# RWKV time mixing on one core: second products of the receptance mix on GpSimd

## The chip, the cores and the metric

The kernel runs on one core of a Trainium2 chip. A core has five engines that run their own instruction queues side by side and meet only at semaphores: TensorE (PE, with its weight loads listed as PEld), VectorE (DVE), ScalarE (ACT), GpSimd (POOL) and SyncE (SP, here only a queue for DMAs). The metric is the device time of one execution in microseconds (us); the figure that counts is the median over several executions. A profile is one execution recorded instruction by instruction. Its span runs from the first to the last instruction and is a little shorter than the time of the same execution.

## What is computed

x has the shape 16 x 2048 x 256 (batch, sequence, channels); all weights are 256 x 256. Cut to what matters:

```python
x_prev[:, 1:, :] = x[:, :-1, :]
xv = x * time_mix_v + x_prev * (1 - time_mix_v)
xr = x * time_mix_r + x_prev * (1 - time_mix_r)
v = xv @ value_weight
r = xr @ receptance_weight
out = ((1 / (1 + np.exp(-r))) * v) @ output_weight
```

The key path of the reference is computed there but not used in its output, and the kernel leaves it out.

## The kernel before

**Tiles.** The 16 x 2048 tokens are cut into 64 units of 512 tokens; four units make a batch entry. x is loaded by DMA from POOL's queue, converted to bf16 (`load`, L103 to L118), and turned by TensorE so that channels lie on the partitions (`transposes`, L197); ACT copies the turned tile from PSUM into `xt` (L225). A tile has 2 halves of channels (`ko` 0 and 1), and each half of a unit has 512 columns. The batch entries 0 and 1 are held unit by unit in `xt_first`; from entry 2 on, `xt` holds the entry as a whole.

**The mix.** With the factor (1 - tm)/tm held in `c_sb`, and tm itself multiplied into the weights, a mix is `c * x_prev + x`. It is made per unit and per m, where m = 0 is R (receptance) and m = 1 is V (value), each called a piece. A piece takes two products, one for each channel half, and one sum over both:

- `scale` (L255) makes a product on DVE (L258, 128 x 512 for one unit, 128 x 1024 for two).
- `scale_pool` (L266) makes the second product (`ko` = 1) on POOL (L268). A dependency written by hand holds it until a given DVE sum is done.
- `scale_act` (L512) makes a product on ACT (L515).
- `add` (L278) makes the sum on DVE (L280, 128 x 1024).

The column of x before a unit's first is not in its own slot; `wrap_slots` (L412) copies it there once per unit or batch entry, by two small copies (L427, L428), before the first product that reads it.

**The main loop** (L523) makes one step per unit g, in this order on the engines: TensorE projects R of unit g (`project`, L288, into psum_r), ACT takes the sigmoid (L536), TensorE transposes units further ahead, DVE makes the products and sums that are due in this step, TensorE projects V (L288, into psum_v), DVE multiplies sigmoid and V into `z_sb` (L581), POOL makes its products, DVE makes the sums that are held back until after z, and TensorE multiplies z of the step before by the output weight (L312, into psum_o), which ACT copies out (L346) and SP's queue stores. psum_r, psum_v and psum_o have one buffer each. The order is written out by hand; no scheduler moves anything.

**Which engine makes which product** is decided in a planning loop (L499 to L510) ahead of the main loop. For each piece, `products[w]` says what DVE makes in step w, and `pooled[w - 1]` which pieces' second product POOL makes in the step before. Before the change, units 10 and later are taken in pairs, and POOL makes the second product of both R and V. Of units 3 to 8 POOL makes the second product of V only; unit 9 has all four on DVE. Unit 1's V product is on POOL and unit 2's second V product on ACT (L563). `AHEAD` is 6 and `PAIRS` is 10. Up to unit 7, a unit's R sum stands in the step before its projection, ahead of z; unit 8's R sum stands after z of step 6. The lines that place POOL's work in a step:

```python
        for p in pooled[g]:                    # L587, after z of step g
            wrap_slots(p, after=last)          # last: the last DVE sum ahead of z
            scale_pool(p, last)
        for p in held[g]:                      # L590
            add(p)
```

So a step's POOL queue holds one wrap copy (L428) and one product, then, where one is due, the issue of a load (L114), and the small copy (L427) of a unit further on.

Of the kernel before, what the change touches and what calls it, by code (L numbers as in the profile page):

```python
# [15 lines left out]
def kernel(  # L16
# [45 lines left out]
    AHEAD = 6  # L62
    PAIRS = 10
# [15 lines left out]
    SYNC = mybir.DependencyInfo(mybir.DependencyClass.Sync, mybir.DependencyReason.DATA)  # L79
# [164 lines left out]
    def slots(piece, off=0):  # L244

        b, _, lo, hi = piece
        j = lo // P + (lo // TU if b < BYUNIT else 0) + off
        return slice(j, j + (hi - lo) // P)

    def mixed(piece):  # L250
        b, m, lo, hi = piece
        j = lo // P % (2 * UJ)
        return mix[(b * S + lo) // (2 * TU)][:, m, j : j + (hi - lo) // P]
# [9 lines left out]
                op0=ALU.mult,  # L263
            )

    def scale_pool(piece, after):  # L266
        b, m, _, _ = piece
        op = nc.gpsimd.tensor_scalar(  # L268
            out=mixed(piece)[:, :, 1],
            in0=xt[b][:, slots(piece), 1],  # L270
            scalar1=c_sb[:, m, 1:2],
            scalar2=1.0,
            op0=ALU.mult,
            op1=ALU.mult,
        )
        tc.add_manual_dep(op.ins, after.ins.name, SYNC, reason="one at a time")

    def add(piece):  # L278
        b = piece[0]
        return nc.vector.tensor_tensor(  # L280
            out=mixed(piece), in0=mixed(piece), in1=xt[b][:, slots(piece, 1)], op=ALU.add
        )
# [13 lines left out]
    def project_unmixed(ps, mo):  # L296


        parts = [(w_prev[:, ko], ko, 0) for ko in range(KO)]
        parts += [(w_bf[:, 0, ko], ko, 1) for ko in range(KO)]  # L300
        for n, (w, ko, lo) in enumerate(parts):
            nc.tensor.matmul(  # L302
                out=ps[:, mo, :],
                lhsT=w[:, mo * P : (mo + 1) * P],
                rhs=xt[0][:, lo : lo + UJ, ko],
                start=(n == 0),
                stop=(n == len(parts) - 1),
            )
# [92 lines left out]
    def tile_for(b):  # L401

        if b not in mix:
            mix[b] = mixpool.tile([P, 2, 2 * UJ, KO, P], BF16, name="mix")

    def pieces(g):

        b, e = divmod(g, UB)
        tile_for(g // 2)
        return [(b, m, e * TU, (e + 1) * TU) for m in range(2)]  # L410

    def wrap_slots(piece, one=None, after=None):  # L412


        b, _, lo, _ = piece
        by_unit = b < BYUNIT
        key = (b, lo // TU if by_unit else UB - 1)
        if key not in late_copies:
            return
        kos = slice(0, KO) if one is None else slice(one, one + 1)  # L420
        if one in (None, KO - 1):
            late_copies.remove(key)
        j = slots(piece).start if by_unit else 0
        n = UJ if by_unit else J
        if by_unit and j > 0:
            engine = nc.vector if key == (0, 1) else nc.gpsimd
            engine.tensor_copy(out=xt[b][:, j, kos, 0:1], in_=xt[b][:, j - 1, kos, P - 1 : P])  # L427
        op = (nc.vector if after is None else nc.gpsimd).tensor_copy(  # L428
            out=xt[b][:, j, kos, 1:P], in_=xt[b][:, j + n, kos, 0 : P - 1]
        )  # L430
        if after is not None:
            tc.add_manual_dep(op.ins, after.ins.name, SYNC, reason="one at a time")
# [4 lines left out]
    def advance(limit):  # L437
        nonlocal tnext, half_load, last_load
        while tnext <= min(limit, NU - 1):
            b, e = divmod(tnext, UB)  # L440
            if b == 1 and e > 0:
                load(b + e + 1)
            elif b > 1 and e == 0 and b + 5 < B:
                if b == 2:
                    load(6)
                last_load = load(b + 5)
                if b + 5 == B - 1:
                    half_load, last_load = last_load
            if tnext < NU - BYDMA:
                transposes(tnext)  # L450
            tnext += 1
# [34 lines left out]
    pooled = {g: [] for g in range(-1, NU)}  # L486
# [12 lines left out]
    for u in range(2, NU):  # L499
        paired = u >= PAIRS  # L500
        if paired and u % 2:
            continue
        for m, (b, _, lo, hi) in enumerate(pieces(u)):
            w = first[u][m]
            group = (b, m, lo, hi + TU if paired else hi)
            if paired or m == 1 and w > 1 and u != PAIRS - 1:
                products[w].append((group, (0,)))
                pooled[w - 1].append(group)
            else:
                products[w].append((group, (0,) if u == 2 and m == 1 else (0, 1)))  # L510

    def scale_act(piece, kos):  # L512
        b, m, _, _ = piece
        for ko in kos:
            nc.scalar.activation(  # L515
                out=mixed(piece)[:, :, ko],
                in_=xt[b][:, slots(piece), ko],
                func=ACT.Copy,
                scale=c_sb[:, m, ko : ko + 1],
            )  # L520

    z_prev2 = z_prev = None
    for g in range(NU - 1):  # L523
        ps_r = ps_r_pool.tile([P, KO, TU], FP32, name="psum_r")
        if g == 0:
            project_unmixed(ps_r, 0)
            advance(1)
            project_unmixed(ps_r, 1)
            for ko in range(KO):
                wrap_slots(pieces(1)[0], ko)  # L530
                scale(pieces(1)[0], (ko,))
            last = add(pieces(1)[0])
        else:
            project(ps_r, g, 0)
        s_sb = zpool.tile([P, KO, TU], BF16, name="s_sb")
        nc.scalar.activation(out=s_sb, in_=ps_r, func=ACT.Sigmoid)  # L536
        advance(START_T[g] if g < len(START_T) else g + LOOK - (g == CROSS - 1))
        for b in range(B - 5, B):
            if g == max(UB * (b - 2) - 1, CROSS + (b > B - 5)):
                new_xt(b)  # L540
                if b == B - 5:
                    for pair in kept.pop(g):
                        store(nc.sync, *pair, after=half_load)
                    by_dma(b, J - UJ, J, last_load)
                    by_dma(b, 0, J - UJ, last_load)
                else:
                    by_dma(b, 0, J)
                for pair in kept.pop(g, []):
                    store(nc.sync, *pair)
            if g == UB * (b - 1) + 1:  # L550
                nc.scalar.copy(out=xt[b][:, 0, :, 1:P], in_=xt[b][:, J, :, 0 : P - 1])
        if LATE_O < g < NU - 2:
            output(g - 2, z_prev2)
        for p in products.get(g + 1, []):
            if g >= FREE and p[0][1] == 1:
                scale_act(p[0], (0,))
        for p in [q for q, _ in products[g]] + pooled[g]:
            last_unit_of = p[3] // TU - 1
            need = last_unit_of if p[0] < BYUNIT else min(last_unit_of + 1, UB - 1)
            assert UB * p[0] + need < tnext, (g, p, tnext)  # L560
            if g > AHEAD or p not in pooled[g]:
                wrap_slots(p)
        if g == 1:  # L563
            scale_act(pieces(2)[1], (1,))
        for p, kos in products[g]:
            if not (g - 1 >= FREE and p[1] == 1):
                scale(p, kos)
        for p in sums[g]:
            last = add(p)
        for p in pooled[g]:  # L570
            if p[0] >= BYUNIT:
                wrap_slots(p)
        ps_v = ps_v_pool.tile([P, KO, TU], FP32, name="psum_v")
        project(ps_v, g, 1)
        if g == 0:
            scale_act(pieces(1)[1], (0,))
            advance(2)
        z_sb = zpool.tile([P, KO, TU], BF16, name="z_sb")
        n = TU // 2 if g == NU - 2 else TU
        for c in range(0, TU, n):  # L580
            nc.vector.tensor_tensor(  # L581
                out=z_sb[:, :, c : c + n],
                in0=s_sb[:, :, c : c + n],
                in1=ps_v[:, :, c : c + n],
                op=ALU.mult,
            )
        for p in pooled[g]:  # L587
            wrap_slots(p, after=last)
# [3 lines that stand above are left out]
        if z_prev is not None and not LATE_O <= g < NU - 3:  # L592
            output(g - 1, z_prev)
        if g == 1:
            advance(4)
        z_prev2, z_prev = z_prev, z_sb
# [31 lines left out]
```

## Time and profile before

| what | value |
|---|---|
| median of 9 runs | 202.75 us (202.41 to 205.46) |
| the profiled execution: its time | 202.58 us |
| the profiled execution: its span | 200.5 us |
| POOL product L268, 128 x 512, mean (6 of xt_first) | 685 ns |
| POOL wrap copy L428, mean | 393 ns |
| DVE product L258, 128 x 512, mean (22 of xt_first) | 349 ns |
| DVE sum L280, mean | 697 ns |
| DVE z L581, mean | 1200 ns |
| ACT product L515, first two (10.75 and 14.24 us) | 0.71 and 0.73 us |
| granted TensorE clock | 0.999 of full |

The page of a profile lists the busy time of each engine, the chain of work that ended last, and the costliest groups by line. A mean is the recorded length of one instruction; on DVE the next one can start before that length is over, so that three products of 349 ns take 0.88 us from the first start to the last end and 0.80 us to the start of what follows. The first 35 us of the span are where single units are used; after that, POOL's product of a pair (128 x 1024) takes 1.1 us.

### The profile page before, as it was taken

Reading aid. Unit: us, or ns where it says so; the run is one execution under the profiler, and the core shown is the slowest. Engines: PE = TensorE matmul, PEld = TensorE weight load, DVE = VectorE, ACT = ScalarE, POOL = GpSimd, SP = SyncE. Lnnn points to the kernel's source line nnn. Section 1 sums busy time; section 2 is a strip of 40 time slices with the busy share of each in tenths; the row PEclk is TensorE's granted clock in tenths of the full one; section 3 lists DMA queues with packets and bytes.
Section 4 is the critical chain, followed back from the end, with each engine's and each line's share of the span. In section 5 each row is a group of like instructions: output and inputs, shape, how many; then the busy total and the mean of one; then the engine's idle time right before and its main releaser. Section 6 shows DMA issues by size and latency. Waiting matters only on the chain.

```text
span 200.5 us, 3886 instructions
## 1 busy us (share of the span) xinstructions
PE 195.0 (97%) x1420; PEld 125.6 (63%) x1420; DVE 186.2 (93%) x296; ACT 180.1 (90%) x202; POOL 83.7 (42%) x115
## 2 busy tenths in 40 slices
PE   8899999999999999999999999999999999999993
PEld 7575676666666666666666666655666565555671
DVE  2799999999999999999999999999999999999982
ACT  3599899999999999999999999899999999999982
POOL 1746572443543534425433354443344444444200
PEclk9999999999999999999999999999999999999999
DMA  5999999999999999999999999999999999999575
GB/s 171 292 167 214 231 280 272 280 282 274 290 314 288 286 280 288 291 273 284 288 286 335 296 412 283 290 176 206 293 270 394 345 220 273 414 420 405 237 310 213
DMA packets 32298, 57.26 MB, mean 286 GB/s; under 512 B 21780, under 2 KB 23064, under 8 KB 28312
## 3 DMA queue, kind: packets, MB, share of 16 engines
q1 hardware_dynamic: 28208, 40.77, 59.3%
q0 software_dynamic: 3920, 16.12, 40.0%
q8 instruction: 11, 0.18, 0.3%
q10 hardware_dynamic: 152, 0.13, 0.2%
q14 instruction: 7, 0.06, 0.1%
HBM read 34.34 MB, written 33.55 MB: 339 GB/s over the span
## 4 chain that ended last, share of the span: by engine, by line
PE 86%; DVE 5%; DMA 3%; issue 2%; ACT 2%; SPq 1%; POOL 0%; DVEq 0%
PE psum_v L288 26%; PE psum_o L312 25%; PE psum_r L288 24%; PE ps_t L209 9%; DMA o_sb<-in_x_dram 3%; DVE z_sb L581 2%; DVE mix L280 2%; PE ps_t L312 1%; DVE mix L258 1%; ACT s_sb L536 1%; ACT mix L515 1%; ACT xt L225 1%; PE ps_t L288 0%; PE psum_r L302 0%; SPq L128 0%
## 5 line engine op out<-in xcount | busy, mean ns | idle before, releaser
L268 POOL TENSOR_SCALAR mix<-xt,c_sb 128x1024 bf16<-128x1024 bf16 (+1 forms) x55 | 61.0, 1109 | 92.6 <-DVE mix L280 79.3
L581 DVE TENSOR_TENSOR z_sb<-s_sb,psum_v 128x1024 bf16<-128x1024 bf16 (+1 forms) x64 | 76.7, 1200 | 3.6 <-PE psum_v L288 1.5
L280 DVE TENSOR_TENSOR mix<-mix,xt 128x1024 bf16<-128x1024 bf16 x112 | 77.0, 697 | 1.6
L288 PEld LDWEIGHTS <-w_bf 128*128 128x128 bf16 x516 | 48.7, 98 | 38.6 <-issue 0.7
L536 ACT ACTIVATE s_sb<-psum_r 128x1024 bf16<-128x1024 f32 x63 | 65.0, 1031 | 3.5 <-PE psum_r L288 2.7
L346 ACT COPY o_sb<-psum_o 128x1024 f32<-128x1024 f32 x60 | 61.1, 1018 | 7.1 <-PE psum_o L312 7.1
L288 PE MATMUL psum_v<-mix,w_bf 128*128 128x512 bf16 (+1 forms) x256 | 65.3, 377 | 0.3 <-DVE z_sb L581 0.2
L288 PE MATMUL psum_r<-mix,w_bf 128*128 128x512 bf16 (+1 forms) x252 | 64.2, 377 | 0.1
L312 PE MATMUL psum_o<-wo_bf,z_sb 128*128 128x256 bf16 x486 | 63.2, 273 | 0.0
L312 PEld LDWEIGHTS <-z_sb 128*128 128x128 bf16 x512 | 49.8, 98 | 20.4 <-issue 1.4
L225 ACT COPY xt<-ps_t 128x1024 bf16<-128x1024 bf16 x36 | 36.6, 1030 | 0.0
L209 PEld LDWEIGHTS <-x_bf 128*128 128x128 bf16 x328 | 21.5, 98 | 8.8
L209 PE MATMUL ps_t<-ident,x_bf 128*128 128x128 bf16 x328 | 24.5, 219 | 0.0
L258 DVE TENSOR_SCALAR mix<-xt,c_sb 128x1024 bf16<-128x1024 bf16 (+1 forms) x49 | 22.1, 459 | 0.0
L515 ACT ACTIVATE mix<-xt,c_sb 128x1024 bf16<-128x1024 bf16 x12 | 13.9, 1157 | 0.0
L280 DVE TENSOR_TENSOR mix<-mix,xt_first 128x1024 bf16<-128x1024 bf16 x15 | 10.6, 709 | 0.1
L114 POOL DMA_DIRECT2D x_bf<-in_x_dram x13 | 8.6, 661 | 0.0
L258 DVE TENSOR_SCALAR mix<-xt_first,c_sb 128x512 bf16<-128x512 bf16 x22 | 6.6, 349 | 0.2
L225 ACT COPY xt_first<-ps_t 128x1024 bf16<-128x1024 bf16 x5 | 5.2, 1036 | 0.0
L268 POOL TENSOR_SCALAR mix<-xt_first,c_sb 128x512 bf16<-128x512 bf16 x6 | 4.1, 685 | 0.9 <-DVE mix L280 0.4
L428 POOL COPY xt_first<-xt_first 128x254 bf16<-128x254 bf16 x5 | 2.0, 393 | 5.5 <-DVE mix L280 5.4
L153 PE MATMUL ps_t<-zeros 128*128 128x128 bf16 x31 | 3.2, 284 | 1.0 <-DVE zeros L90 1.0
(66 smaller groups left out, 51.4 us busy)
## 6 DMA issues: line engine op xcount, KB each, us to landing
out_dram<-o_sb SPq DMA_DIRECT2D x28, 1024.0 KB, 14.1
x_bf<-in_x_dram POOLq DMA_DIRECT2D x13, 1024.0 KB, 23.4
out_dram<-o_sb SPq DMA_DIRECT2D x4, 512.0 KB, 2.8
out_dram<-o_sb SPq DMA_DIRECT2D x6, 256.0 KB, 2.5
x_bf<-in_x_dram POOLq DMA_DIRECT2D x5, 256.0 KB, 7.0
o_sb<-in_x_dram SPq DMA_DIRECT2D x2, 512.0 KB, 5.5
x_bf<-in_x_dram POOLq DMA_DIRECT2D x2, 512.0 KB, 10.8
o_sb<-in_x_dram SPq DMA_DIRECT2D x2, 256.0 KB, 2.8
```

What stands on the lines that cost most here:

```text
L114: return nc.gpsimd.dma_start(out=x_bf[b], in_=rows(b), max_dma_last_dim=run)
L209: nc.tensor.transpose(out=ps[:, jj], in_=src[:, jj, ko * P : (ko + 1) * P], identity=idn)
L225: nc.scalar.copy(out=xt[b][:, j0 : j0 + UJ], in_=ps)
L258: nc.vector.tensor_scalar(out=mixed(piece)[:, :, ko], in0=xt[b][:, slots(piece), ko], scalar1=c_sb[:, m, ko : ko + 1], scalar2=None, op0=A ...
L268: op = nc.gpsimd.tensor_scalar(out=mixed(piece)[:, :, 1], in0=xt[b][:, slots(piece), 1], scalar1=c_sb[:, m, 1:2], scalar2=1.0, op0=ALU.mul ...
L280: return nc.vector.tensor_tensor(out=mixed(piece), in0=mixed(piece), in1=xt[b][:, slots(piece, 1)], op=ALU.add)
L288: nc.tensor.matmul(out=ps[:, mo, :], lhsT=w_bf[:, m, ko, mo * P : (mo + 1) * P], rhs=mixed((b, m, e * TU + lo, e * TU + hi))[:, :, ko], st ...
L312: nc.tensor.matmul(out=ps[:, slot, :], lhsT=z[:, ko, jj * P : (jj + 1) * P], rhs=wo_bf[:, ko, :], start=(ko == 0), stop=(ko == KO - 1),)
L346: nc.scalar.copy(out=o_sb[b][:, j0 : j0 + UJ, :], in_=ps)
L515: nc.scalar.activation(out=mixed(piece)[:, :, ko], in_=xt[b][:, slots(piece), ko], func=ACT.Copy, scale=c_sb[:, m, ko : ko + 1],)
L536: nc.scalar.activation(out=s_sb, in_=ps_r, func=ACT.Sigmoid)
L581: nc.vector.tensor_tensor(out=z_sb[:, :, c : c + n], in0=s_sb[:, :, c : c + n], in1=ps_v[:, :, c : c + n], op=ALU.mult,)
```

## The change

R's pieces of units 3 to 8 are treated as V's: DVE makes the first product, POOL the second. In POOL's list R's piece comes ahead of V's, so that the wrap copy comes with R's. For unit 8 both POOL products stand in step 6, and its wrap copy stays on DVE. The second V product of unit 2 goes from ACT to POOL, in step 1, without the dependency on a DVE sum. Unit 9 and the pairs are as before.

```diff
-    def scale_pool(piece, after):
+    def scale_pool(piece, after=None):
         b, m, _, _ = piece
         op = nc.gpsimd.tensor_scalar(
...
-        tc.add_manual_dep(op.ins, after.ins.name, SYNC, reason="one at a time")
+        if after is not None:
+            tc.add_manual_dep(op.ins, after.ins.name, SYNC, reason="one at a time")
...
-            if paired or m == 1 and w > 1 and u != PAIRS - 1:
+            if paired or w > 1 and u != PAIRS - 1:
                 products[w].append((group, (0,)))
-                pooled[w - 1].append(group)
+                at = w if m == 0 and u == AHEAD + 2 else w - 1
+                pooled[at].insert(0 if m == 0 else len(pooled[at]), group)
             else:
                 products[w].append((group, (0,) if u == 2 and m == 1 else (0, 1)))
...
-            if g > AHEAD or p not in pooled[g]:
+            if g > AHEAD or p not in pooled[g] or p == pieces(AHEAD + 2)[0]:
                 wrap_slots(p)
         if g == 1:
-            scale_act(pieces(2)[1], (1,))
+            scale_pool(pieces(2)[1])
```

## The prediction

> **What bounds the kernel now.** I read the page's shares and chain first, then a table of windows cut at the first weight load of each step's R projection, then the timeline of DVE and POOL. "Step g" is one turn of the main loop, "unit u" the 512 tokens projected in step u; R and V are the two mixes of a unit.
>
> ```profile
> PE 195.0 (97%) x1420; PEld 125.6 (63%) x1420; DVE 186.2 (93%) x296; ACT 180.1 (90%) x202; POOL 83.7 (42%) x115
> PE 86%; DVE 5%; DMA 3%; issue 2%; ACT 2%; SPq 1%; POOL 0%; DVEq 0%
> ```
> TensorE carries the end for most of the span, POOL for none. DVE's 5% is where this change can act; the windows say where.
>
> ```profile
> core 0: us, PE busy (x) PEld busy (x) DVE busy (x) ACT busy (x) POOL busy (x), PEclk, DMA share, GB/s
> 11.26:14.92 3.66, 3.66 (x34) 2.52 (x33) 3.55 (x8) 3.65 (x7) 1.42 (x4) 1.00 1.05 179
> 14.92:18.01 3.09, 3.09 (x27) 1.97 (x25) 3.08 (x7) 3.09 (x5) 1.65 (x5) 1.00 1.13 216
> 18.01:21.29 3.28, 3.22 (x27) 2.02 (x24) 3.28 (x7) 3.28 (x4) 2.02 (x5) 1.00 1.05 212
> 21.29:24.54 3.25, 3.22 (x26) 2.01 (x24) 3.04 (x7) 2.92 (x4) 2.00 (x5) 1.00 1.07 232
> 24.54:28.04 3.50, 3.50 (x35) 2.46 (x33) 3.50 (x7) 3.19 (x4) 3.31 (x7) 1.00 1.04 276
> 28.04:31.66 3.62, 3.62 (x35) 2.46 (x32) 3.62 (x10) 3.62 (x5) 0.87 (x2) 1.00 1.06 278
> 31.66:35.02 3.36, 3.12 (x26) 1.97 (x24) 3.36 (x7) 3.36 (x4) 1.36 (x3) 1.00 1.06 278
> 35.02:38.51 3.49, 3.49 (x34) 2.46 (x32) 3.49 (x7) 3.19 (x5) 1.11 (x1) 1.00 1.04 277
> 38.51:41.56 3.05, 3.05 (x27) 2.01 (x24) 2.94 (x6) 3.05 (x4) 1.12 (x1) 1.00 1.06 278
> ```
> The rows are steps 1 to 9; the first number after the window is its length. A step with eight transposes needs 3.05 us of TensorE (step 9), one with sixteen 3.49 (step 8). Steps 1 to 7 took 3.66, 3.09, 3.28, 3.25, 3.50, 3.62 and 3.36 where 3.49, 3.05, 3.05, 3.05, 3.49, 3.49 and 3.05 were needed: 1.09 us lost in all. That is the most a faster DVE can give back, since from step 8 on TensorE is full. DVE is busy throughout these steps. One of them in the timeline, DVE and POOL:
>
> ```profile
> 19.52 0.88 DVE L258 TENSOR_SCALAR mix<-xt_first,c_sb 128x512 bf16<-128x512 bf16 x3
> 20.32 0.68 DVE L280 TENSOR_TENSOR mix<-mix,xt_first 128x1024 bf16<-128x1024 bf16 x1
> 20.92 1.21 DVE L581 TENSOR_TENSOR z_sb<-s_sb,psum_v 128x1024 bf16<-128x1024 bf16 x1
> 21.13 0.39 POOL L428 COPY xt_first<-xt_first 128x254 bf16<-128x254 bf16 x1 [1.15 <-DVE mix L280]
> 21.62 0.68 POOL L268 TENSOR_SCALAR mix<-xt_first,c_sb 128x512 bf16<-128x512 bf16 x1
> 22.05 0.80 DVE L280 TENSOR_TENSOR mix<-mix,xt_first 128x1024 bf16<-128x1024 bf16 x1
> 22.27 0.76 POOL L114 DMA_DIRECT2D x_bf<-in_x_dram  x1
> ...
> 25.59 0.68 DVE L280 TENSOR_TENSOR mix<-mix,xt_first 128x1024 bf16<-128x1024 bf16 x1
> ...
> 27.02 0.73 POOL L427 COPY xt_first<-xt_first 128x2 bf16<-128x2 bf16 x1
> 27.03 0.67 DVE L280 TENSOR_TENSOR mix<-mix,xt_first 128x1024 bf16<-128x1024 bf16 x1
> ```
> Start to start, DVE spends 0.80 on three scales, 0.60 on the R add, 1.13 on z, 0.72 on the V add: 3.25 at most, 3.17 where nothing waits. Note when POOL works: it starts 0.13 us after the R add, and wrap copy and product lie under z, which reads PSUM.
>
> **What the skill says.** The Trainium skill, page "SBUF — State Buffer", section "Who interferes with whom": DVE and GpSimd share one SBUF port pair; a DVE instruction in a two-port mode, or with two SBUF inputs, contends with a GpSimd instruction that reads SBUF, and whichever comes second "fully blocks" until the first is done; a DVE instruction with one SBUF input outside those modes doesn't contend. The trace agrees. The V add lasts 0.68 us where the POOL product ended before it (25.59, product done at 25.56), and 0.80 where the product overlaps it by 0.25 (22.05, product until 22.30); the adds at 15.51 (overlap 0.27, 0.80 us), 18.88 (0.18, 0.71) and 28.76 (0.25, 0.80) fit too: the add gets its port about 0.15 before the product's recorded end. In the other direction, a POOL copy of two columns takes 0.20 us alone (23.03) and 0.73 beside an add (27.02): it ended 0.05 after the add. z, one input from PSUM, never suffered from a product. That a DVE scale contends is the page's claim ("VectorE: DVE Perf Modes", section "Mode 4×_2P — both tricks at once": bf16 scaling uses both read ports); no run here shows one beside a POOL product.
>
> **The change, part by part.**
>
> Removed from DVE: the second product of R in steps 2 to 6: one scale in each of steps 2 to 5, two in step 6 (units 7 and 8). One costs 0.27 start to start (0.80/3): 6 x 0.27 = 1.6 us. Against the measured z starts: z1 at 14.38 to z5 at 27.63 took 13.25, which includes 0.1 and 0.3 of waits for ACT at z2 and z4. With two scales a turn is 0.53 + 0.60 + 1.13 + 0.72 = 2.98, four of them 11.92: 1.33 gained; step 6, 4.50 between z5 and z6, loses two scales, 0.53. Together 1.86 us before any new stall.
>
> Removed from ACT: one activation of 0.73 (14.24) in step 1. The copy behind it (14.86) moves up only to when its PSUM is ready, some 14.75: 0.1 gain for the sigmoid of step 2, behind which z2 no longer stands. Nothing on the path.
>
> Added to POOL: seven products of 0.68 (row of 128x512). The R product comes first, behind the wrap copy that its piece now carries; the count of copies is unchanged. The V product and what follows it in POOL's queue (memset, the load's issue of 0.76, the next wrap copy of 0.20) move 0.68 later per step. The V product ended 3 us before its V add (19.06 against 22.05), so that is hidden. The loads land 14.5 to 36.6 us after issue behind a DMA queue that is already full (DMA share 1.04 to 1.13), and no instruction of TensorE or ACT waits for a load's landing after 8 us: hidden. POOL's own load per step becomes 0.39 + 0.68 + 0.68 + 0.76 + 0.20 plus 0.23 of gaps = 2.9, under the turn of 3.05; step 4, with two load issues (1.47), is over it.
>
> Added wait: the R add waits for POOL's R product. It starts 0.62 after the preceding R add's end and is done at 1.30; the next R add is due some 2.6 later. No stall.
>
> Added collisions, the part that decides. From the end E of the R add: copy E+0.13 to 0.52, R product E+0.62 to 1.30, V product from E+1.26. z covers only to E+1.05. So the R product overlaps the V add as the V product does today (0.1, already in the 0.72), and the V product meets the V add head on. I take it that the add, waiting first, runs from E+1.15 to about E+1.73, and the V product, waiting since E+1.3, then gets the port before the next step's scales. It was already dispatched, so it holds the port for less than its 0.68 - 0.15 = 0.53: 0.43 if it moves 512 elements at the rate that the 0.43 us between the 1.11 us and 0.68 us products imply. Against this stands DVE's own gap of some 0.05 between two instructions. Block x = 0.40 us per step; bounds 0 (POOL fits between DVE's accesses) and 0.67 (the V product keeps the port from the R product on: it would end at E+1.98, so the add starts at 1.83 instead of 1.15, with no block after). It falls in steps 2 to 6, that is five times up to z6. (Unit 8's pair delays the V-side of step 7 by 0.25, where there is slack.) Unit 2's product is a sixth: it becomes ready with DVE's wrap copy at 12.88, just as three scales start (12.99), with the R add and z1 behind them: 0.40 again.
>
> Sum: 6x - 1.86 us at z6, with the gain cut off at 1.09. At x = 0.40: 2.40 - 1.86 = +0.54. It reaches the end in full: the V projection of step 7 waits for z6 already (33.39, PSUM has one buffer), and after it TensorE has no slack. The profiled execution took 202.58 (span 200.5 and 2.1 around it), so 203.1; the median shown is 0.17 above it: 203.3.
>
> **The rivals.**
>
> 1. Lock as above, x from 0.31 to 0.5: +0.0 to +1.1, centre 203.3. For: both directions of blocking are in the trace. Against: no POOL product stands beside a scale in it. Chance 0.55.
>
> 2. Back-to-back products hold the port, x = 0.67: 6 x 0.67 - 1.86 = +2.2, 204.9. A POOL queue that runs late in step 4 (two load issues) and delays R7's add ends near here too. For: POOL's next instruction starts 0.04 before the last ends (22.27 against 22.30). Against: the add asks first. 0.15.
>
> 3. The other side: blocks stay under 0.1, because a scale of 0.27 leaves the port free in part (the POOL copies at 19.78 and 23.03 took 0.20 beside scales, and the scales 0.87 as ever). Then 6x - 1.86 lies beyond the cut and TensorE becomes the bound in steps 2 to 7: -1.0, 201.7. It decides from x under 0.31. Against: those copies move two columns; a product needs the port for 0.4 us. 0.17.
>
> 4. Gains and blocks cancel, x near 0.30, or ACT, whose queue runs without a gap from 24.85 to 32.99 (nine instructions), hides what is left: within 0.3 of 202.75. 0.13.
>
> **How the numbers follow.** Time 203.3, of the likeliest case. A change of 0.2% (0.4 us) is about what a measurement of this kernel can tell. Faster: rival 3 and a little of 4, 0.17. Same: most of 4 and the lower part of 1 (x under 0.38), 0.24. Slower: the rest of 1 and rival 2, 0.59. The range 201.9 to 204.9 leaves out about half of rivals 2 and 3; the likeliest case's own range is 202.7 to 203.9.
>
> **What would show it.** In the changed profile: z starts 3.3 to 3.45 apart in steps 2 to 5 (right), 3.05 (rival 3) or 3.6 and more (rival 2); a gap of about 0.4 between V add and the first scale, or a stretched first scale, with a POOL product over it; POOL products longer than 0.68 where they wait; the scales of step 1 spread by a POOL product at 13.0; the step windows 4 and 7 longer than 3.25 and 3.36. I'd be wrong if scales and products overlap with neither stretched, or if steps 8 and later change.

## The result, and the profile after

The changed kernel takes 204.38 us (median of 16 executions, 203.82 to 207.15); the kernel before takes 202.77 us over all the executions made beside it. The ratio is 1.0082, with a 95% interval from 1.0064 to 1.0100: 1.3 to 2.0 us slower. One of the 16 executions (207.15 us, clock 0.989) was in a slower state of the chip and is left out of the ratio. The predicted 203.3 us is 1.1 too low: the time lies within the stated range of 201.9 to 204.9, but above the likeliest case's own (to 203.9), and the change is three times the forecast +0.5.

The profiled execution of the changed kernel took 205.56 us, its span 203.5. The first lines to compare are the busy times and the shares of the chain of waits, from its page:

```profile
PE 196.8 (97%) x1420; PEld 126.6 (62%) x1420; DVE 188.4 (93%) x290; ACT 179.7 (88%) x201; POOL 90.4 (44%) x122
...
PE 76%; DVE 13%; issue 4%; ACT 3%; DMA 2%; POOL 0%; SPq 0%; DVEq 0%; POOLq 0%
```

DVE lost six instructions (296 to 290) and is busy 2.2 us longer (186.2 to 188.4). An instruction that is held counts as busy (below, a scale of 0.35 us is recorded with 0.78), so the lost time stands inside the busy time. DVE's share of the chain went from 5% to 13%, TensorE's from 86% to 76%. POOL still has 0%: it delays DVE and never ends the chain itself.

The table of windows, cut as before at the first weight load of each step's R projection, steps 1 to 9:

```profile
core 0: us, PE busy (x) PEld busy (x) DVE busy (x) ACT busy (x) POOL busy (x), PEclk, DMA share, GB/s
12.53:16.30 3.77, 3.74 (x35) 2.57 (x34) 3.66 (x8) 3.31 (x6) 1.87 (x4) 1.00 1.09 196
16.30:19.79 3.49, 3.13 (x28) 1.94 (x26) 3.49 (x6) 3.49 (x4) 2.94 (x5) 1.00 1.10 218
19.79:23.25 3.46, 3.22 (x27) 2.01 (x24) 3.46 (x6) 2.89 (x4) 3.22 (x6) 1.00 1.05 208
23.25:26.66 3.41, 3.22 (x26) 2.01 (x24) 3.37 (x6) 2.84 (x3) 3.22 (x5) 1.00 1.03 231
26.66:30.16 3.50, 3.50 (x35) 2.46 (x33) 3.50 (x6) 3.19 (x4) 3.39 (x5) 1.00 1.05 284
30.16:34.05 3.89, 3.76 (x35) 2.46 (x32) 3.89 (x8) 3.89 (x5) 2.74 (x6) 1.00 1.06 273
34.05:37.41 3.36, 3.11 (x23) 1.97 (x24) 3.36 (x7) 3.10 (x4) 2.02 (x4) 1.00 1.04 280
37.41:40.91 3.50, 3.50 (x35) 2.46 (x33) 3.50 (x7) 3.19 (x4) 1.11 (x1) 1.00 1.05 275
40.91:44.57 3.66, 3.20 (x27) 2.04 (x24) 3.56 (x7) 3.32 (x4) 1.12 (x1) 1.00 1.05 280
```

Window by window against before, in us: +0.11, +0.40, +0.18, +0.16, 0, +0.27, 0, +0.01, +0.61; in sum +1.74. From the end of step 9 to the end of the span both kernels take 158.9 us. The span of this one execution also holds 1.27 us that lie ahead of step 1 (12.53 against 11.26). In part that is a load of x for which TensorE waited until 5.24 us, where it went on at 4.44 before; over all profiles below, z of step 0 starts anywhere from 10.6 to 12.3 us. Without the 1.27 us its 205.56 would be 204.29, close to the median. So the whole loss lies in steps 1 to 9, and a third of it in step 9, in which the change alters no instruction. The clock was 1.00 throughout and the DMA share hardly moved.

Now the rows of DVE and POOL in the timeline, step 1 and the turn from step 3 to step 4:

```profile
14.33 1.31 DVE L258 TENSOR_SCALAR mix<-xt_first,c_sb 128x512 bf16<-128x512 bf16 x3
14.39 0.85 POOL L268 TENSOR_SCALAR mix<-xt_first,c_sb 128x512 bf16<-128x512 bf16 x1 [1.01 <-DVE xt_first L429]
15.56 0.68 DVE L281 TENSOR_TENSOR mix<-mix,xt_first 128x1024 bf16<-128x1024 bf16 x1
...
20.33 1.78 POOL L268 TENSOR_SCALAR mix<-xt_first,c_sb 128x512 bf16<-128x512 bf16 x2
20.75 0.80 DVE L281 TENSOR_TENSOR mix<-mix,xt_first 128x1024 bf16<-128x1024 bf16 x1
21.48 0.78 DVE L258 TENSOR_SCALAR mix<-xt_first,c_sb 128x512 bf16<-128x512 bf16 x1
22.44 0.68 DVE L281 TENSOR_TENSOR mix<-mix,xt_first 128x1024 bf16<-128x1024 bf16 x1
```

In step 1 three scales take 1.23 us to the start of the R add (14.33 to 15.56) where they took 0.80: POOL's product of unit 2 stands over them and is itself stretched from 0.68 to 0.85. In step 3 POOL's R and V products (20.33 to 22.11) take 1.78 instead of twice 0.68. The R product delays the V add as the V product did before (0.80 recorded), the V add holds the V product, and the V product holds the first scale: 0.78 us for an instruction of 0.35. Two scales take 0.96 to the R add instead of 0.53.

### The profile page after: what moved, and what is told of

The parts are those of the page before. It is cut to its first block, busy times and chain, and to the rows that moved or that the text cites. A ratio compares the mean times of both kernels' runs of the same rounds, so it can differ in the third digit from the quotient of the medians.

```text
span 203.5 us, 3893 instructions
## 1 busy us (share of the span) xinstructions
PE 196.8 (97%) x1420; PEld 126.6 (62%) x1420; DVE 188.4 (93%) x290; ACT 179.7 (88%) x201; POOL 90.4 (44%) x122
## 4 chain that ended last, share of the span: by engine, by line
PE 76%; DVE 13%; issue 4%; ACT 3%; DMA 2%; POOL 0%; SPq 0%; DVEq 0%; POOLq 0%
PE psum_v L289 22%; PE psum_o L313 22%; PE psum_r L289 21%; PE ps_t L209 6%; DVE z_sb L583 5%; DVE mix L281 5%; DVE mix L258 3%; DMA o_sb<-in_x_dram 2%; PE ps_t L313 1%; ACT s_sb L538 1%; ACT xt L225 1%; PE psum_r L303 1%; PE psum_v L232 1%; PE ps_t L153 1%; ACT mix L517 1%
## 5 line engine op out<-in xcount | busy, mean ns | idle before, releaser
L268 POOL TENSOR_SCALAR mix<-xt,c_sb 128x1024 bf16<-128x1024 bf16 (+1 forms) x56 | 61.7, 1101 | 91.0 <-DVE mix L281 81.2
L268 POOL TENSOR_SCALAR mix<-xt_first,c_sb 128x512 bf16<-128x512 bf16 x12 | 10.6, 892 | 2.8 <-DVE mix L281 1.3
L258 DVE TENSOR_SCALAR mix<-xt_first,c_sb 128x512 bf16<-128x512 bf16 x17 | 8.2, 521 | 0.2
L153 PE MATMUL ps_t<-zeros 128*128 128x128 bf16 x31 | 3.7, 313 | 1.0 <-DVE zeros L90 1.0
L218 ACT CAST xt_first<-ps_t 128x512 bf16<-128x512 f32 x4 | 2.1, 587 | 2.4 <-PE ps_t L209 2.4
```

The source lines that it names most:

```text
L258: nc.vector.tensor_scalar(out=mixed(piece)[:, :, ko], in0=xt[b][:, slots(piece), ko], scalar1=c_sb[:, m, ko : ko + 1], scalar2=None, op0=A ...
L268: op = nc.gpsimd.tensor_scalar(out=mixed(piece)[:, :, 1], in0=xt[b][:, slots(piece), 1], scalar1=c_sb[:, m, 1:2], scalar2=1.0, op0=ALU.mul ...
```

## The experiments

The theory on record is a port held in turn: POOL's second product of a step takes the read port from the next scale of DVE, and each such block costs more than the 0.27 us that a removed scale gives back. Its rivals: the R add waits for POOL's product (a dependency, no port); TensorE or ACT bounds these steps anyway; and, for step 9, something behind step 6 that the prediction had as slack.

As a common measure I use the time from the start of z of step 0 to the start of z of step 9, from each profile, against the 30.75 us of before. It leaves out the start-up. Two profiles of one kernel differ in it by 0.04 us (the changed kernel) and 0.19 us (early_u8, 0.16 of it in step 2), so small differences are not read from it. "Measured" is the ratio to the kernel before, run on the same chip beside it.

| kernel | z0 to z9, change in us | of it up to z6 | measured ratio (95% interval) | median us, before beside it |
|---|---|---|---|---|
| the changed kernel | +1.74 | +1.06 | 1.0082 (1.0064 to 1.0100) | 204.38, 202.77 |
| after_again | +1.78 | +1.08 | 1.0067 (1.0036 to 1.0099) | 204.48, 202.93 |
| after_pad | +1.44 | +1.09 | 1.0078 (1.0058 to 1.0099) | 204.38, 202.88 |
| u2_on_act | +1.00 | +0.65 | 1.0052 (1.0026 to 1.0079) | 203.82, 202.81 |
| only_u2 | +0.46 | +0.45 | 1.0018 (1.0000 to 1.0036) | 203.20, 202.81 |
| r3_to_6 | +0.78 | +0.78 | 1.0031 (1.0010 to 1.0051) | 203.61, 202.93 |
| left_out | -0.94 | -0.96 | 0.9959 (0.9940 to 0.9978) | 202.20, 202.81 |
| spare | +2.77 | +2.44 | 1.0136 (1.0102 to 1.0171) | 205.46, 202.81 |
| write_only | +1.47 | +1.47 | 1.0096 (1.0064 to 1.0127) | 204.93, 202.88 |
| early | -0.41 | -0.29 | 0.9993 (0.9969 to 1.0018) | 203.12, 202.93 |
| change_early | +0.06 | +0.13 | 0.9999 (0.9977 to 1.0021) | 202.85, 202.88 |
| early_u8 | -0.49 | -0.42 | 0.9975 (0.9952 to 0.9998) | 202.14, 202.93 |
| early_u8_again | -0.68 | -0.61 | 0.9964 (0.9952 to 0.9976) | 202.18, 202.88 |

The two columns agree within the intervals: what these nine steps gain or lose is, as far as the intervals can tell, what the kernel gains or loses.

### The parts of the change

**u2_on_act** is the changed kernel with unit 2's product back on ACT.

```diff
-            scale_pool(pieces(2)[1])
+            scale_act(pieces(2)[1], (1,))
```

> The change without its second part: unit 2's second V product is on ScalarE again, the R products of units 3 to 8 stay on GpSimd. Port theory: the three scales of step 1 take 0.80 us to the R add again instead of 1.23, so 0.4 us come back: 203.9 to 204.1, about 1.2 us over the kernel before, with steps 2 to 9 as in the changed kernel (3.49, 3.46, 3.41, 3.50, 3.89, 3.36, 3.50, 3.66). Rival, that the R add's new wait for GpSimd's product is what costs and unit 2's product is free: no difference from the changed kernel, 204.4.

The three scales of step 1 are back at 0.80 us (13.22 to 14.02), z0 to z1 fell from 3.90 to 3.46, and the rest up to z6 is as in the changed kernel. Step 9's window is 3.33 us, not 3.66. The time, 203.82, is just under the 203.9 to 204.1 expected.

**only_u2** is the kernel before with this one edit.

```diff
-            scale_act(pieces(2)[1], (1,))
+            scale_pool(pieces(2)[1])
```

> The kernel before with only unit 2's second V product moved from ScalarE to GpSimd. Port theory: scales of step 1 spread from 0.80 to about 1.2 us, z of step 1 some 0.4 late, and VectorE has no slack up to step 7 but for the 0.1 and 0.3 us it waits for ScalarE at z of steps 2 and 4, part of which absorbs it: 202.9 to 203.2. Rival, that it is free: 202.7, or a little less for the relief of ScalarE.

The scales of step 1 take 1.23 again (13.25 to 14.48), z0 to z1 takes 3.90, and the delay is 0.45 at z6 and 0.46 at z9. Both runs give this edit a price of 0.4 us up to z6 (0.45 alone; 1.06 - 0.65 in the other), and what it takes off ACT gives nothing back: z2 regains 0.08 us, and z3 loses it again. The interval of only_u2's ratio reaches down to 1.

**r3_to_6** keeps R's products of units 3 to 6 on POOL, and leaves units 2, 7 and 8 as before.

```diff
-            if paired or w > 1 and u != PAIRS - 1:
+            if paired or w > 1 and u != PAIRS - 1 and (m == 1 or u <= 6):
```

> Only the R products of units 3 to 6 are on GpSimd; units 7 and 8 and unit 2 are as before. Port theory: z of steps 2 to 5 as in the run with unit 2 on ScalarE (13.74 us from z of step 1 to z of step 5, 13.25 before), then step 6 and the V side of step 7 as before (4.50 and 3.12): 0.4 to 0.5 us over before, 203.2. If the loss lies in step 6 and later, where GpSimd's queue with its two load issues runs late: within 0.2 of before.

z0 to z9 is 0.78 longer, all of it before z6; from z6 on the intervals are those of before (3.12, 3.36, 3.07). In step 6 the V product still starts late (29.38, 1.16 us after z5, where it took 0.71 before; recorded 1.27 us), and the three scales beside it take 1.14 instead of 0.80 (30.09 to 31.23), though no R product of unit 7 is there. So the late start is enough for one block in step 6; the cause of the lateness is in the answer to the prediction below. This missed the expectation, which had step 6 as before (4.50) and 203.2 us: z5 to z6 is 4.74, and the time 203.61. Step 6 even loses more here (+0.24) than in u2_on_act (+0.15), which has the blocks but is also rid of two scales.

**left_out** leaves R's second products of units 3 to 8 out of the computation, with zeros in their place, and unit 2 on ACT.

```diff
+        return spare[u % 2] if m == 0 and 3 <= u <= 8 else mixed(piece)
...
-            scale_pool(p, last)
+            if p[1] or p[0] * UB + p[2] // TU >= PAIRS:
+                scale_pool(p, last)
```

> The second products of R of units 3 to 8 are left out: the sum takes zeros in their place, so these units' R mix lacks the share of the previous column in its second half of channels. Unit 2 is on ScalarE. VectorE saves what it saves in the changed kernel and GpSimd has nothing more to do than before. Port theory: steps 2 to 4 go to about 3.05 and steps 6 and 7 shrink, 0.7 to 1.05 us faster than before, 201.7 to 202.1. If VectorE's time did not matter in these steps (TensorE or ScalarE as the bound): 202.5 or more.

This is the gain without the price: -0.94 us at z9, and the ratio says -0.4 to -1.2. Steps 3 and 4 ran at 3.02 and 3.05 from z to z, about what TensorE alone needs (3.05). The gain fits the limit of 1.09 us in the prediction; the time, 202.20, is 0.1 above the expected 201.7 to 202.1. The instructions that the change takes off DVE were worth about 0.9 us; the price was more.

### A port or a wait

**spare** lets DVE keep all its products. POOL makes the R products as in the changed kernel, into a tile that nobody reads, so no instruction of DVE waits for them.

```diff
-            out=mixed(piece)[:, :, 1],
+            out=mixed(piece)[:, :, 1] if m or b * UB + piece[2] // TU >= PAIRS else spare,
...
-                products[w].append((group, (0,)))
+                extra = not paired and m == 0
+                products[w].append((group, (0, 1) if extra else (0,)))
```

> VectorE keeps both products of R of units 3 to 8, and GpSimd makes the second one as well, into a spare tile that nobody reads; unit 2 is on ScalarE. So GpSimd works as in the changed kernel, nothing waits for its extra product, and VectorE saves nothing. Port theory: the first scales of steps 2 to 5 are held some 0.43 us each, those of step 6 up to 0.77, the V side of step 7 0.33; with what the waits at z absorb 2.0 to 3.0 us over before, 204.8 to 205.8. Rival, that the wait of the R add for GpSimd's product costs: nothing waits here, so 202.8.

The timeline of this run, DVE and POOL, around the turn from step 2 to step 3:

```profile
18.64 0.68 POOL L269 TENSOR_SCALAR spare<-xt_first,c_sb 128x512 bf16<-128x512 bf16 x1
19.06 0.80 DVE L282 TENSOR_TENSOR mix<-mix,xt_first 128x1024 bf16<-128x1024 bf16 x1
19.31 1.11 POOL L269 TENSOR_SCALAR mix<-xt_first,c_sb 128x512 bf16<-128x512 bf16 x1
19.78 1.43 DVE L259 TENSOR_SCALAR mix<-xt_first,c_sb 128x512 bf16<-128x512 bf16 x3
20.37 0.75 POOL L115 DMA_DIRECT2D x_bf<-in_x_dram  x1
21.13 0.67 DVE L282 TENSOR_TENSOR mix<-mix,xt_first 128x1024 bf16<-128x1024 bf16 x1
```

The picture of the changed kernel returns, though no instruction of DVE waits for POOL's R product: the V product is stretched to 1.11 us by the V add, and the scales take 1.35 us to the R add (19.78 to 21.13) instead of 0.80. The wait as a cause falls; the port stays. The time, 205.46, is within the 204.8 to 205.8 expected. The block is 0.55 here against 0.43 in the changed kernel. The third of the three scales by itself shows where the rest lies:

```profile
20.75 0.47 DVE L259 TENSOR_SCALAR mix<-xt_first,c_sb 128x512 bf16<-128x512 bf16 x1
```

The V product holds the first scale by 0.44 us (recorded with 0.78), as in the changed kernel. The other 0.12 is in this third scale, which starts 0.38 us into POOL's load issue (20.37) and is recorded with 0.47. In spare and write_only all eight third scales that start 0.37 to 0.39 us into a load issue take 0.47 to 0.48, and in step 5 of spare, with no load issue beside it, the third scale takes 0.34. In steps 2 to 5 of the changed kernel no third scale is there. Whether a load issue holds the scale at the same port, no run shows.

**write_only** is the kernel before with a memset of 128 x 1024 bf16 on POOL behind the V product, one in each of steps 1 to 6, into a tile that nobody reads. The memset only writes; the trace lists no input for it.

```diff
+        if any(p[1] == 0 and p[0] * UB + p[2] // TU < PAIRS for p in pooled[g]):
+            nc.gpsimd.memset(spare, 0.0)
```

> VectorE and GpSimd do what they did before, and in steps 1 to 6 GpSimd sets a spare tile of 128 x 1024 bf16 to zero behind the V product: work that only writes. What the skill's SBUF page says: the V add, which reads two inputs and writes through its own port, is not held by it (0.80 us as ever), the scales, in a two-port mode, are; then the first scale of steps 2 to 6 is stretched until the memset ends and the kernel is 0.5 to 2 us slower. If only the read port is contended: neither is stretched, 202.8. If any GpSimd work holds VectorE: the add is stretched too.

Its timeline, DVE and POOL, step 2 to 3, and then the sum behind z of step 6:

```profile
20.10 0.80 DVE L282 TENSOR_TENSOR mix<-mix,xt_first 128x1024 bf16<-128x1024 bf16 x1
20.32 0.94 POOL L596 MEMSET spare<- 128x1024 bf16 x1
20.82 1.24 DVE L259 TENSOR_SCALAR mix<-xt_first,c_sb 128x512 bf16<-128x512 bf16 x3
21.21 0.76 POOL L115 DMA_DIRECT2D x_bf<-in_x_dram  x1
21.98 0.67 DVE L282 TENSOR_TENSOR mix<-mix,xt_first 128x1024 bf16<-128x1024 bf16 x1
...
35.42 0.95 POOL L596 MEMSET spare<- 128x1024 bf16 x1
35.67 0.68 DVE L282 TENSOR_TENSOR mix<-mix,xt 128x1024 bf16<-128x1024 bf16 x1
```

The sum at 20.10 lies beside the memset for 0.58 us and takes 0.80 us; that is what V adds took before where the V product overlapped them by 0.25, as it does here. The sum at 35.67 lies wholly beside a memset and takes 0.68, where beside a POOL product the changed kernel's takes 1.01 (35.66). The six memsets take 0.94 to 0.95. The scales behind the sum take 1.16 to the R add, 0.36 more than 0.80: 0.24 is in the first, which is recorded with 0.58 and ends 0.15 after the memset, and 0.12 in the third, beside the load issue as in spare. So the two kinds of DVE instruction are told apart. The Trainium skill, "SBUF — State Buffer", section "Who interferes with whom", says just this: two SBUF inputs contend with a GpSimd instruction that reads, "not with one that only writes it", while a two-port mode contends with any. Nobody waits for the memset, and the kernel is 0.6 to 1.3% slower all the same.

### Step 9

**after_again** is the changed kernel once more.

> The changed kernel once more, for a second profile. In the first one GpSimd's product for units 10 and 11 came 0.52 us after the sum it follows, and step 9 took 3.66 us instead of 3.05. If this belongs to the change, it is there again; if it was this execution, that product comes 0.1 to 0.2 after its sum and step 9 takes 3.3 or less, as in the run with unit 2 on ScalarE. The scales of steps 1 to 6 (1.23, 1.00, 0.96, 0.96, 0.97, 1.57 us to the sum) are the same in either case.

All intervals from z to z recur within 0.01 us, step 9 with 3.68 us, and so does a gap that is read below: 0.52 us between the end of a sum and the POOL product that waits for it.

**after_pad** adds four tiny memsets at the program's start, which do nothing for the computation and move POOL's later instructions back in its program.

```diff
+    pad = consts.tile([P, 4], BF16)
+    for n in range(4):
+        nc.gpsimd.memset(pad[:, n : n + 1], 0.0)
```

> The changed kernel with four tiny memsets more in GpSimd's idle start, which move every later GpSimd instruction four places down its program. In both profiles of the changed kernel GpSimd's product for units 10 and 11 began 0.52 us after the sum it waits for (0.1 to 0.2 elsewhere, and 0.17 there with unit 2 on ScalarE, where it stands one place earlier), and step 9 took 3.66 and 3.68 us. If the gap hangs on the place in the program, it is gone from this product (0.2 or less) and step 9 takes 3.3: 0.3 us less, 204.1. If it comes from the change's timing, it is there again and the time is as before, 204.4.

The gap is 0.18 us (sum done at 36.49, product from 36.67), z7 to z8 falls from 3.70 to 3.35, and step 9 takes 3.33 us. The median did not follow: 204.38, on four executions. So in these profiles the gap goes with the place of the instruction in POOL's program; the expected 204.1 us did not come. That the gap costs the kernel time outside the profiled execution is not shown, and what it is was not found.

### Starting POOL's work earlier

If z hides only what POOL finds time for under it, POOL should start as z starts. **early** is the kernel before with POOL's copy and product released by the DVE instruction ahead of the last sum before z, not by that sum. POOL then waits for the port beside the sum.

```diff
-                scale(p, kos)
-        for p in sums[g]:
+                ahead = scale(p, kos)
+        for n, p in enumerate(sums[g]):
+            ahead = last if n else ahead
...
-            wrap_slots(p, after=last)
-            scale_pool(p, last)
+            point = ahead if 1 <= g <= PAIRS - 2 else last
+            wrap_slots(p, after=point)
+            scale_pool(p, point)
```

> The kernel before, but GpSimd's wrap copy and V product of steps 1 to 8 wait for the VectorE instruction ahead of the sum instead of the sum itself, so that they stand ready when the sum gives the port back. Port theory: they start some 0.2 us earlier and are done before the V add, which takes 0.68 us instead of 0.80 in steps 1, 3, 5 and 7; VectorE gains 0.1 us in each: 0.2 to 0.4 us faster, 202.4 to 202.6. Risk in the same theory: if GpSimd gets the port before the sum does, each sum is held 0.2 to 0.4 us and the kernel is 0.5 to 1.5 us slower. If the order of waiting has no effect: 202.8.

Step 3 in the timeline, DVE and POOL:

```profile
20.67 0.68 DVE L281 TENSOR_TENSOR mix<-mix,xt_first 128x1024 bf16<-128x1024 bf16 x1
20.89 0.72 POOL L429 COPY xt_first<-xt_first 128x254 bf16<-128x254 bf16 x1 [0.87 <-ACT s_sb L537]
...
22.41 0.68 DVE L281 TENSOR_TENSOR mix<-mix,xt_first 128x1024 bf16<-128x1024 bf16 x1
```

Every V add now takes 0.68 us; in steps 2 to 5 the wrap copy is recorded with 0.72 to 0.73 instead of 0.39, since it comes to the port while the sum runs and waits, and the sum keeps its 0.68. The z starts gain 0.41 us. The time did not show it: the median is 203.12, not 202.4 to 202.6, and the interval, from -0.6 to +0.4 us, contains both the expected gain and none at all.

**change_early** is the changed kernel with this release and with unit 2 on ACT.

> The R products of units 3 to 8 on GpSimd, unit 2 on ScalarE, and GpSimd's work of steps 1 to 8 waits for the VectorE instruction ahead of the sum. Port theory: the V product then ends some 0.3 us sooner; it stands in the way of the V add alone (about 0.4 us) and no longer of the add by 0.1 and the scales by 0.43: turns of 3.3 us instead of 3.42 in steps 2 to 5, and in all about 0.5 us less than with unit 2 on ScalarE alone (203.8): 203.3. It can't be faster than before, since one hold of 0.43 is more than the 0.27 saved. If the order of waiting has no effect on the collision: 203.8.

202.85 us, level with before and 0.45 better than expected: the second product's block is 0.35 to 0.36 us in steps 2, 4 and 5 (23.92 to 24.81 for two scales in step 4) and 0.43 in step 3, where a load issue made POOL late, and the V adds take 0.68 to 0.72. In steps 2 and 4 the waiting product let the first scale pass as well (0.34) and held the second (0.70). The loss of R's products of units 3 to 8 (u2_on_act: +0.5%) is gone, and so is their gain: a turn still has a block larger than the 0.27 of a scale removed, and z5 to z6 still takes 4.65.

**early_u8** is early with one part of the change: unit 8's R product on POOL, in step 6.

```diff
-            if paired or m == 1 and w > 1 and u != PAIRS - 1:
+            if paired or w > 1 and u != PAIRS - 1 and (m == 1 or u == AHEAD + 2):
```

> The same, and of R's second products only unit 8's on GpSimd, in step 6, where VectorE has the most to do and GpSimd no wrap copy. Port theory: two products with a port hold of 0.43 us each, started as the last sum ends, fit under z of step 6 (1.13 us), so VectorE saves 0.27 us there at no cost, on top of the gain of the early start: 0.4 to 0.7 us faster than before, 202.1 to 202.4. Rival, that any R product on GpSimd costs time: not faster than the run with the early start alone.

The timeline of step 6 in this run, DVE and POOL:

```profile
30.57 1.29 DVE L282 TENSOR_TENSOR mix<-mix,xt_first 128x1024 bf16<-128x1024 bf16 x2
31.43 1.66 POOL L269 TENSOR_SCALAR mix<-xt,c_sb 128x512 bf16<-128x512 bf16 x2 [2.65 <-ACT xt L225]
31.78 1.21 DVE L585 TENSOR_TENSOR z_sb<-s_sb,psum_v 128x1024 bf16<-128x1024 bf16 x1
32.91 0.72 DVE L282 TENSOR_TENSOR mix<-mix,xt 128x1024 bf16<-128x1024 bf16 x1
```

POOL was free for 2.65 us ahead of the pair, so both products could be issued during the sum (31.43). They are done at 33.09, and all but the last 0.18 us lies under the sum and z. The R add behind z pays 0.04 (0.72), not 0.33 as in the changed kernel, and DVE has one scale fewer: z5 to z6 takes 4.12 us instead of 4.50 before and 4.39 in early. **early_u8_again** repeats it.

> The kernel with the early start and unit 8's R product on GpSimd once more, for its time: 0.4 to 0.8 us faster than before, as in the first run (202.14 against 202.93).

202.14 and 202.18 us, against 202.93 and 202.88 for the kernel before beside them: 0.25% (0.02 to 0.48) and 0.36% (0.24 to 0.48) faster. This version beats both kernels. DVE has 2% of its chain of waits in both profiles, against 5% before. Which share the early start has in it and which the product wasn't separated by times: in the z starts, of the 0.49 to 0.68 us, the product gives 0.27 in step 6 and costs 0.05 in step 7 (z6 to z7 3.17 for 3.12).

## Why the prediction went as it did

**The bound.** Right. The loss stands in the steps in which DVE is full, and left_out gave 0.94 us where the prediction had 1.09 as the most that DVE can give.

**The mechanism.** Right: rival 1, the port held in turn. (So DVE and POOL do not meet only at semaphores, as the introduction has it.) The time alone would not say so: 204.4 is nearer to rival 2's 204.9 than to rival 1's 203.3. The trace does: the V add runs between the two products (20.75 in the result), so they don't keep the port from one to the next. POOL products longer than 0.68 us, a stretched first scale, scales of step 1 spread by a product, z starts 3.31 to 3.53 apart in steps 2 to 5 (3.3 to 3.45 forecast; the 3.53 is step 4, where it was 3.54 before and z still waits for more than the R add), windows 4 and 7 at 3.41 and 3.36. The window of step 7 was forecast longer than 3.36, and was not. One reading of the lines was off: the two-column copy at 23.03, said to take 0.20 us "alone", ran beside scales, as rival 3 has it; it takes 0.18 beside z (11.86 in the kernel before).

**The size of one block.** Nearly right. The term was 0.40 us: a hold of 0.43 less a gap of DVE's own. Measured, as the time from the first scale to the R add less 0.80 (three scales) or 0.53 (two): 0.43 in step 1, 0.47 in step 2, 0.43 in steps 3, 4 and 5. So the hold was right, and the gap took nothing off.

**The count of blocks up to z6.** This step failed. "It falls in steps 2 to 6, that is five times up to z6", and unit 2's makes six. There were seven. Step 6 in the timeline, POOL from the end of step 5, then DVE and POOL:

```profile
28.90 1.48 POOL L114 DMA_DIRECT2D x_bf<-in_x_dram  x2
...
30.53 0.41 POOL L429 COPY xt_first<-xt_first 128x254 bf16<-128x254 bf16 x1
31.04 1.26 POOL L268 TENSOR_SCALAR mix<-xt_first,c_sb 128x512 bf16<-128x512 bf16 x1
31.75 0.70 DVE L258 TENSOR_SCALAR mix<-xt_first,c_sb 128x512 bf16<-128x512 bf16 x1
32.29 0.71 POOL L268 TENSOR_SCALAR mix<-xt_first,c_sb 128x512 bf16<-128x512 bf16 x1
32.37 0.78 DVE L258 TENSOR_SCALAR mix<-xt_first,c_sb 128x512 bf16<-128x512 bf16 x1
33.07 0.34 DVE L258 TENSOR_SCALAR mix<-xt,c_sb 128x512 bf16<-128x512 bf16 x1
```

Two load issues in a row (28.90 to 30.38) held POOL's queue. The wrap copy started at 30.53, 0.65 us into z (29.88), where z had been meant to cover copy and R product. So z covered neither product: the R product held one scale (0.70) and the V product the next (0.78). The three scales took 1.57 us instead of 0.80, a block of 0.77. The prediction had noticed that POOL's load in the step with two issues was over the length of a turn, and in rival 2 that the queue "runs late"; but it let that delay unit 7's R add, which it didn't, and not double the block, which it did. With 0.43 + 0.47 + 0.43 + 0.43 + 0.43 + 0.77 = 2.96 us the prediction's own sum gives 2.96 - 1.86 = +1.10 at z6; measured +1.06, forecast +0.54. r3_to_6 shows the lateness by itself: with one product in step 6 there is one block.

**The parts costed at nothing.** Right for the dependency of the R add on POOL (in spare the V product's block is there without it, 0.44 us) and for the activation taken from ACT (only_u2).

**What comes after z6.** This failed too, in a half sentence: unit 8's pair "delays the V-side of step 7 by 0.25, where there is slack", and from step 8 on nothing was to change; a change there was named as a sign of being wrong, and step 9 took 0.61 us longer. POOL's pair and the R add behind z of step 6:

```profile
34.77 1.36 POOL L268 TENSOR_SCALAR mix<-xt,c_sb 128x512 bf16<-128x512 bf16 x2 [1.77 <-DVE mix L281]
35.66 1.01 DVE L281 TENSOR_TENSOR mix<-mix,xt 128x1024 bf16<-128x1024 bf16 x1
```

The pair held the R add behind z6 for 0.33 us (35.66 to 36.59, 0.93 to the next start where 0.60 is usual), and z7 came 0.34 later still. Without this pair and without unit 7's R product (r3_to_6) the interval z6 to z7 is 3.12 as before, and with the pair started early (early_u8) 3.17. Then the step from 8 to 9:

```profile
37.39 0.68 DVE L281 TENSOR_TENSOR mix<-mix,xt 128x1024 bf16<-128x1024 bf16 x1
...
38.59 1.11 POOL L268 TENSOR_SCALAR mix<-xt,c_sb 128x1024 bf16<-128x1024 bf16 x1 [1.79 <-DVE mix L281]
39.12 1.12 DVE L281 TENSOR_TENSOR mix<-mix,xt 128x1024 bf16<-128x1024 bf16 x1
...
41.69 1.20 DVE L583 TENSOR_TENSOR z_sb<-s_sb,psum_v 128x1024 bf16<-128x1024 bf16 x1
...
42.94 1.02 PE L289 MATMUL psum_v<-mix,w_bf 128*128 128x512 bf16 x4 [0.46 <-DVE z_sb L583]
```

POOL's product of the first pair of units waits for the sum that ends at 38.06 and starts at 38.59, the gap of 0.52 us. In u2_on_act it starts 0.17 us after its sum. The later start pushes it from under z onto unit 9's R add, which takes 1.04 to the next start (39.12 to 40.16) instead of the 0.70 it takes in u2_on_act. z8 is then 1.74 us late while TensorE, whose steps 1 to 8 grew by 1.13, is less so; the V projection of step 9 finds psum_v still being read and waits 0.46 us. After that TensorE has no slack to make anything up with. Where the gap is absent (u2_on_act, after_pad), step 9 still takes 3.33: the delay that z7 has by then is enough to reach it.

**The sum.** +0.54 forecast; in the profile +1.74: +0.52 from the blocks up to z6 (0.19 their size, 0.37 the seventh block, less 0.04 that the sum doesn't explain), +0.34 from unit 8's pair, +0.34 from the gap, whose cost outside the profiles is not shown. The measured times say +1.3 to +2.0. The sign and the mechanism were right, and the value too small because POOL's late queue was seen and not carried into the next step, and because slack behind z6 was taken for granted and not counted.

## What to carry to other kernels

An engine that shares a port with a full one is free only under the instructions that don't use the port: here z, 1.13 us, less the 0.6 us that POOL needed to get to its product. One product of 0.68 is nearly hidden there (it costs the V add 0.1), and the second costs more (0.43) than it removes (0.27). Before giving such an engine more, lay its whole queue, load issues too, against those windows in every step, and count a block for each product that falls outside. And let it start by waiting for the port, queued beside the instruction that holds it, rather than by a semaphore after that instruction: that alone turned a kernel that loses into one that is level, and made room for the one product that gained.

## What the runs showed of the hardware

- A wait for the port stands inside the recorded length of the waiting instruction, on either engine: a POOL product of 0.68 us was recorded with up to 1.26, a scale of 0.35 with 0.70 to 0.78, a copy of 0.39 with 0.72. Busy time and means by group don't tell it from work.
- A POOL copy or product that comes to the port while DVE's sum runs waits and costs that sum nothing (0.68 us in every case of early).
- A POOL memset, which reads nothing, held a DVE scale for 0.24 us (write_only, step 2) and left the sum of two SBUF inputs alone (0.68 us wholly beside it).
- A DVE scale that starts 0.37 to 0.39 us into a load issue of POOL is recorded with 0.47 to 0.48 us instead of 0.34 (spare and write_only, eight cases).
- The start of a POOL product after the sum that it waits for took 0.52 us in two profiles of the changed kernel, and 0.18 once four tiny instructions had been put at the program's start. What it is, no run shows.
